# An added one-column memset as VectorE's first instruction, in a streaming multiply and GELU

## The chip, the cores and the metric

One core of one Trainium2 chip runs the kernel. The metric is the device time in microseconds (us), the median of several executions. The profile has a span as well: the time from the first to the last of the program's own instructions in one profiled execution. Time and span are not the same number, and both are given below. The engines are VectorE (DVE in the profile), ScalarE (ACT), GpSimd (POOL), SyncE (SP) and TensorE (PE, which has no work here). Transfers between HBM and the on-chip memory are issued by SP, ACT or POOL and carried out by 16 DMA engines.

## The reference

```python
batch, dim = 1024, 4096          # x and y: float32
z = x * y
out = 0.5 * z * (1 + np.tanh(np.sqrt(2 / np.pi) * (z + 0.044715 * z ** 3)))   # float32
```

Two inputs of 16.8 MB are read, and one output of 16.8 MB is written. Each element is multiplied once and goes through one GELU in its tanh form.

## The kernel before

The arrays are taken as one flat run of 4,194,304 numbers, laid out over 128 partitions, so that each partition has 32,768 columns. `PIECES` cuts the columns into three pieces: 1,280, 16,384 and 15,104 of them. Each piece is contiguous in HBM.

All of x stays in the buffer `xs` (128 x 32,768), where the product and then the GELU overwrite it in place. y goes through a smaller buffer `ys` of 20,440 columns. The y pieces are loaded in the order of `Y_LOADS`: the second piece to column 4,056 of `ys`, then the third to column 0, then the first to column 15,104. The last two overwrite columns that the multiplies of the first have read.

The program is written out by hand, engine by engine, with semaphores. Nothing schedules it.

- SP issues the load of the first x piece (L73), waits for it, then issues the first y load (L77) and the third x piece. The second y load waits for three multiplies (and for the semaphore of the 68-byte load, below), the third for four. Then SP issues the three stores (L124), each when the last GELU of its piece is done, waits for them, and clears the semaphores (L126 to L130).
- ACT issues the load of the second x piece (L73), and then runs one GELU (L115) behind each multiply.
- VectorE runs the multiplies (L107): four of 4,096 columns, seven of 2,048, one of 768 and one of 1,280. The first waits for the first y load and the second x piece (L104).
- GpSimd issues one small load (L83): 17 numbers, 68 bytes, of y to columns 0 to 16 of `ys` in partition 0. They are overwritten by the second y load before anything reads them.

Ahead of these instructions every program has a start stage, which the kernel's framework writes (L145 in the profile): GpSimd fills four constants of one column each with a MEMSET, every engine drains, and a barrier gathers the engines before it releases them. Two more barriers follow (L60). The function `_hoist` takes an instruction from where it was issued and puts it ahead of the start stage of its own engine, in front of that engine's first drain or memset:

```python
    at = next(
        k
        for k, i in enumerate(first)
        if i.engine == engine and type(i).__name__ in ("InstDrain", "InstMemset")
    )
    first[at:at] = issued
```

Three instructions are hoisted: the first x load on SP, the second x load on ACT, and the 68-byte load on GpSimd. So these three stand in front of the first barrier; GpSimd's stands in front of the four constants too. VectorE's first instruction is its drain.

Of the kernel before, what the change touches and what calls it, by code (L numbers as in the profile page):

```python
# [1 line left out]

# [4 lines left out]


F32 = mybir.dt.float32
GELU = mybir.ActivationFunctionType.Gelu_apprx_tanh  # L10

PIECES = [(0, 1280), (1280, 17664), (17664, 32768)]

Y_LOADS = [(1280, 17664, 4056), (17664, 32768, 0), (0, 1280, 15104)]

Y_FREE = [0, 3, 4]

STEPS = [[4096] * 4, [2048] * 7 + [768], [1280]]  # L20
STORES = [(1280, 17664), (17664, 32768), (0, 1280)]
Y_BUF = 20440
SPARE = 0


def _hoist(nc, issued):

    here = nc.cur_bb.bb.instructions
    first = nc.main_func.blocks[0].instructions
    for ins in issued:  # L30
        del here[next(k for k, i in enumerate(here) if i is ins or i.name == ins.name)]
    engine = issued[0].engine
# [8 lines that stand above are left out]
@with_exitstack  # L41
def kernel(
    ctx: ExitStack,
    tc: tile.TileContext,
    x: bass.AP,
    y: bass.AP,
    out: bass.AP,
):
    nc = tc.nc
    P = nc.NUM_PARTITIONS  # L50

    def columns(t, a, b):

        flat = t.flatten_outer_dims().rearrange("r c -> (r c)")
        pa, pb = next(q for q in PIECES if q[0] <= a and b <= q[1])
        return flat[P * pa : P * pb].rearrange("(p c) -> p c", p=P)[:, a - pa : b - pa]


    tc.close()
    tc.compile()  # L60

    xs = nc.alloc_sbuf_tensor("xs", [P, PIECES[-1][1]], F32).ap()
    ys = nc.alloc_sbuf_tensor("ys", [P, Y_BUF], F32).ap()
    sem_x = [nc.alloc_semaphore(f"sem_x{i}") for i in range(len(PIECES))]
    sem_y = [nc.alloc_semaphore(f"sem_y{i}") for i in range(len(Y_LOADS))]
    sem_s = nc.alloc_semaphore("sem_s")
    sem_mul = nc.alloc_semaphore("sem_mul")
    sem_act = nc.alloc_semaphore("sem_act")
    sem_o = [nc.alloc_semaphore(f"sem_o{i}") for i in range(len(STORES))]

    def load_x(i, engine=nc.sync):
        a, b = PIECES[i]
        return engine.dma_start(out=xs[:, a:b], in_=columns(x, a, b)).then_inc(sem_x[i], 16)  # L73

    def load_y(i):
        a, b, r = Y_LOADS[i]
        return nc.sync.dma_start(  # L77
            out=ys[:, r : r + b - a], in_=columns(y, a, b)
        ).then_inc(sem_y[i], 16)

    _hoist(nc, [load_x(0).ins])
    _hoist(nc, [load_x(1, nc.scalar).ins])
    spare = nc.gpsimd.dma_start(  # L83
        out=ys[0:1, SPARE : SPARE + 17], in_=columns(y, 0, 17)[0:1, :]
    ).then_inc(sem_s, 16)
    _hoist(nc, [spare.ins])
    nc.sync.wait_ge(sem_x[0], 16)
    load_y(0)
    load_x(2)
    for i in range(1, len(Y_LOADS)):  # L90
        if Y_FREE[i]:
            nc.sync.wait_ge(sem_mul, Y_FREE[i])
        if i == 1:
            nc.sync.wait_ge(sem_s, 16)
        load_y(i)

    nc.scalar.wait_ge(sem_x[0], 16)
    n = 0
    done = {}
    for i, (a, b, r) in enumerate(Y_LOADS):  # L100
        for j, (xa, xb) in enumerate(PIECES):
            if xa <= a < xb:
                nc.vector.wait_ge(sem_x[j], 16)
        nc.vector.wait_ge(sem_y[i], 16)  # L104
        c = a
        for w in STEPS[i]:
            nc.vector.tensor_mul(  # L107
                out=xs[:, c : c + w],
                in0=xs[:, c : c + w],
                in1=ys[:, r + c - a : r + c - a + w],  # L110
            ).then_inc(sem_mul, 1)
            n += 1
            done[c + w] = n
            nc.scalar.wait_ge(sem_mul, n)
            nc.scalar.activation(  # L115
                out=xs[:, c : c + w], in_=xs[:, c : c + w], func=GELU
            ).then_inc(sem_act, 1)
            c += w

    for i, (a, b) in enumerate(STORES):  # L120
        if i == 0:
            nc.sync.wait_ge(sem_y[-2], 16)
        nc.sync.wait_ge(sem_act, done[b])
        nc.sync.dma_start(out=columns(out, a, b), in_=xs[:, a:b]).then_inc(sem_o[i], 16)  # L124
    for i in range(len(STORES) - 1):
        nc.sync.wait_ge(sem_o[i], 16)  # L126
    nums = sorted(s.num for s in [*sem_x, *sem_y, *sem_o[:-1], sem_s, sem_mul, sem_act])
    assert nums == list(range(nums[0], nums[-1] + 1))
    nc.sync.sem_clear(range(nums[0], nums[-1] + 1))
    nc.sync.wait_ge(sem_o[-1], 16).then_inc(sem_o[-1], -16)  # L130


# [1 line left out]
_INS = ['x', 'y']  # L134
_OUTS = [((1024, 4096), 'float32')]


# [23 lines left out]
```

## Time and profile before

| what | value |
|---|---|
| time, median of 3 runs | 119.35 us (119.30 to 119.42) |
| time of the profiled execution | 119.36 us |
| span of the profiled execution | 118.5 us |
| VectorE busy | 35.2 us, 13 instructions |
| ScalarE busy | 30.9 us, 14 instructions |
| GpSimd busy | 0.8 us, 5 instructions |
| moved by DMA | 50.33 MB, mean 425 GB/s over the span |
| VectorE's first multiply starts | 42.68 us |
| the 68-byte load, from issue to landing | 10.0 us |

Zero of all profile times is the span's start, which is the start of SP's first load. The page gives each engine's busy time, and the same in 40 equal slices as tenths, with the share of the DMA engines below. The chain that ended last is followed back from the last instruction to what released it, step by step. A timeline row gives start, length, engine, source line, operation and output<-input. A "q" behind an engine's name marks its sequencer, which waits, drains and issues transfers; such rows are not counted as busy time. The one DMA issue that counts as busy is GpSimd's.

### The profile page before, as it was taken

How to read it: one execution, taken by the hardware profiler on the slowest of the kernel's cores; microseconds unless marked ns; L12 is line 12 of the kernel's file. 1: busy time of each engine (PE TensorE's matmuls, PEld its weight loads, DVE VectorE, ACT ScalarE, POOL GpSimd, SP SyncE). 2: the span in 40 equal slices, each digit the busy share in tenths (PEclk: the TensorE clock that was granted, in tenths of full speed). 3: DMA queues.
4: the chain of work that ended last, by engine and by line, in shares of the span. 5: the costliest groups of instructions: out<-in, count | busy, mean ns of one | idle time of the engine just before them, and what ended most of it. 6: DMA issues, size and time to landing. Idle time of an engine off the chain costs nothing.

```text
span 118.5 us, 85 instructions
## 1 busy us (share of the span) xinstructions
DVE 35.2 (30%) x13; ACT 30.9 (26%) x14; POOL 0.8 (1%) x5
## 2 busy tenths in 40 slices
DVE  0000000000000059999920000059999940000000
ACT  0000000000000000999975000006998990000000
POOL 2000000000000000000000000000000000000000
DMA  9888899889988897798797797798899887977975
GB/s 464 381 382 382 381 553 509 354 354 420 641 354 354 354 632 347 326 632 347 326 632 347 326 632 347 326 575 354 354 531 531 354 354 326 652 326 326 652 326 221
DMA packets 1328, 50.33 MB, mean 425 GB/s; under 512 B 176, under 2 KB 176, under 8 KB 560
## 3 DMA queue, kind: packets, MB, share of 16 engines
q1 hardware_dynamic: 1152, 41.94, 82.2%
q10 hardware_dynamic: 144, 8.39, 16.6%
q0 software_dynamic: 32, 0.00, 0.0%
HBM read 33.55 MB, written 16.78 MB: 425 GB/s over the span
## 4 chain that ended last, share of the span: by engine, by line
DMA 55%; DVE 24%; ACT 3%; issue 1%; DVEq 0%
DMA ys<-in_y_dram 41%; DVE xs L107 24%; DMA xs<-in_x_dram 13%; ACT xs L115 3%; DVEq L104 0%
## 5 line engine op out<-in xcount | busy, mean ns | idle before, releaser
L107 DVE TENSOR_TENSOR xs<-xs,ys 128x2048 f32<-128x2048 f32 (+3 forms) x13 | 35.2, 2778 | 60.9 <-DMA ys<-in_y_dram 60.9
L115 ACT ACTIVATE xs<-xs 128x2048 f32<-128x2048 f32 (+3 forms) x13 | 29.6, 2300 | 19.6 <-DVE xs L107 19.6
L115 ACT ACT_TABLE_LOAD x1 | 1.3, 1283 | 47.2 <-DVE xs L107 47.2
L83 POOL DMA_DIRECT2D ys<-in_y_dram x1 | 0.6, 632 | 0.7 <-issue 0.7
L145 POOL MEMSET const-bfloat16-1.0<- 128x1 bf16 x1 | 0.1, 130 | 0.0
L145 POOL MEMSET const-uint8-127<- 128x1 uint8 x1 | 0.1, 130 | 0.0
L145 POOL MEMSET const-float32-0.0<- 128x1 f32 x1 | 0.1, 128 | 0.0
L145 POOL MEMSET const-float32-1.0<- 128x1 f32 x1 | 0.1, 127 | 0.0
## 6 DMA issues: line engine op xcount, KB each, us to landing
xs<-in_x_dram SPq DMA_DIRECT2D x1, 7552.0 KB, 44.0
ys<-in_y_dram SPq DMA_DIRECT2D x1, 7552.0 KB, 22.5
out_dram<-xs SPq DMA_DIRECT2D x1, 7552.0 KB, 20.4
xs<-in_x_dram SPq DMA_DIRECT2D x1, 640.0 KB, 16.0
ys<-in_y_dram SPq DMA_DIRECT2D x1, 640.0 KB, 19.7
out_dram<-xs SPq DMA_DIRECT2D x1, 640.0 KB, 20.8
xs<-in_x_dram ACTq DMA_DIRECT2D x1, 28.0
ys<-in_y_dram POOLq DMA_DIRECT2D x1, 0.1 KB, 10.0
```

Source lines behind the costliest of these rows:

```text
L83: spare = nc.gpsimd.dma_start(out=ys[0:1, SPARE : SPARE + 17], in_=columns(y, 0, 17)[0:1, :]).then_inc(sem_s, 16)
L107: nc.vector.tensor_mul(out=xs[:, c : c + w], in0=xs[:, c : c + w], in1=ys[:, r + c - a : r + c - a + w],).then_inc(sem_mul, 1)
L115: nc.scalar.activation(out=xs[:, c : c + w], in_=xs[:, c : c + w], func=GELU).then_inc(sem_act, 1)
L145: nc = _bacc.Bacc("TRN2", target_bir_lowering=False, num_devices=1)
```

## The change

One constant and one line are added. VectorE gets a memset of column 32 of `ys` (128 partitions, one float32 each, value 0), hoisted to the front of VectorE's instructions, ahead of its first drain. Column 32 is not among the columns 0 to 16 of the 68-byte load, and the second y load overwrites it before a multiply reads it. All other engines keep their instructions and the order of them; GpSimd's first is still the 68-byte load. The two added lines shift the line numbers by one or two.

```diff
 Y_BUF = 20440
+EARLY = 32
 SPARE = 0
...
+    _hoist(nc, [nc.vector.memset(ys[:, EARLY : EARLY + 1], 0.0).ins])
     _hoist(nc, [load_x(0).ins])
     _hoist(nc, [load_x(1, nc.scalar).ins])
     spare = nc.gpsimd.dma_start(
```

## The prediction

> **What bounds the kernel now.** I read the page first (busy shares and the 40 slices), then the chain that ended last, then the timeline of the first two microseconds, then the rows of the line that holds the start barrier. All times below are microseconds from the start of the span unless a duration is meant.
>
> The slices of the page (busy tenths by engine, then the share of the 16 DMA engines):
>
> ```profile
> span 118.5 us, 85 instructions
> DVE  0000000000000059999920000059999940000000
> ACT  0000000000000000999975000006998990000000
> POOL 2000000000000000000000000000000000000000
> DMA  9888899889988897798797797798899887977975
> ```
>
> The reader is to see that DMA is busy from the first slice to the last, while VectorE (DVE) works in two islands, and does nothing at all in the first 14 slices. The kernel is a stream of 50.33 MB through the DMA engines. Its interior can only change if the transfers start later, or if a transfer is held back.
>
> The chain that ended last (start, length, what) begins with three transfers or waits on transfers:
>
> ```profile
> 0.00 15.99 DMA xs<-in_x_dram
> 15.99 0.02 issue
> 16.01 26.57 DMA ys<-in_y_dram
> ```
>
> So the first row on which anything depends is SP's load at 0.00, and nothing else of the first 15.99 us is on the path. VectorE's first multiply follows at 42.68, when the large y load has landed.
>
> The timeline of the start (start, length, engine, line, operation):
>
> ```profile
> 0.00 0.39 SPq L73 DMA_DIRECT2D xs<-in_x_dram  x1
> 0.12 0.36 ACTq L73 DMA_DIRECT2D xs<-in_x_dram  x1
> 0.74 0.63 POOL L83 DMA_DIRECT2D ys<-in_y_dram  x1 [0.74 <-issue]
> 1.35 0.13 POOL L145 MEMSET const-float32-0.0<- 128x1 f32 x1
> 1.39 0.13 POOL L145 MEMSET const-float32-1.0<- 128x1 f32 x1
> 1.42 0.13 POOL L145 MEMSET const-bfloat16-1.0<- 128x1 bf16 x1
> 1.46 0.13 POOL L145 MEMSET const-uint8-127<- 128x1 uint8 x1
> ```
>
> The reader is to see that three DMA issues stand before the first instruction in which a compute engine writes anything: GpSimd's MEMSET at 1.35 (1.355 in the trace). VectorE has no row here.
>
> And the barrier that ends this stage, in the rows of line 145 (ns min/median/max, first and last start):
>
> ```profile
> L145 DVEq DRAIN  x1: 10/10/10, 0.1 to 0.1; - x1
> L145 POOLq DRAIN  x1: 10013/10013/10013, 0.8 to 0.8; - x1
> ```
>
> VectorE reaches the barrier at 0.12 and stands there until GpSimd's drain, 10.01 long, ends at 10.83.
>
> **The clock's own ends.** The profiled execution has a time of 119.36, its span is 118.53. The time is 0.83 longer, so it isn't the span, and where it begins has to be inferred. If it begins at t, it ends at 119.36 + t. The trace has semaphore records behind the span: resets of single semaphores from 118.80 to 119.41, then a chain of nine hand-offs around the engines from 119.63 to 119.99. A clock that began with SP's load at 0.00 would end at 119.36, in the middle of the resets, where no engine has just finished. A clock that began with GpSimd's DMA row (0.738) would end at 120.10, which is 0.11 behind the last hand-off. One that began with GpSimd's first MEMSET (1.355) would end at 120.715, which is 0.73 behind it. I take the last. DMA_DIRECT2D is the same operation in the first three rows, so a rule by which it opens the clock would have opened it at 0.00; the first row that is certainly work of a compute engine is the MEMSET.
>
> The Trainium skill bears on both ends. Its page "Perfetto Trace Analysis" (section "GPSIMD Engine Instruction") says that a GpSimd instruction that reads no tensor has no reported start, so that 0.738 may not be a start at all; no run here shows it. Its page "Runtime: NRT & Kernel Launch" (section "The ~15µs preamble/postamble breakdown") lists, behind the kernel, a barrier, semaphore resets and a second barrier with a re-arming of the DMA rings, some 5 us in sum; by that figure the end would be an estimated 123.5 and the start 4.2, where nothing of the first rows begins, and the trace's resets, 0.61 long against its 1.5, disagree with it.
>
> **The change part by part.** It adds one instruction, VectorE's memset of one column (128x1 f32) of ys. It removes and moves nothing: the other four engines have the same instructions in the same order, and SP's and ACT's loads are still the first of their queues.
>
> - Its own work: the nearest row is GpSimd's MEMSET of 128x1 f32, 0.13. VectorE has no work before 42.68, so it costs nothing there.
> - VectorE's arrival at the barrier: its DRAIN now stands behind the memset. It would be late by some 0.07 to start and 0.13 to run, so at about 0.32 in place of 0.12. The barrier is gathered at 10.87, behind GpSimd's 10.01 drain: 10.5 of slack. Without that cover the 0.2 would go to the next wait, SP's for x piece 0 from 11.67 to 15.99, which hides 4.3 more. Cost nothing.
> - Transfers: column 32 lies outside the 68-byte load (columns 0 to 16) and is written next by the y load issued at 55.80. No wait is added, and nothing queues behind the memset but the barrier. Cost nothing.
> - GpSimd: whether a VectorE memset can hold up GpSimd's rows isn't in the trace. Between 0 and one memset, 0.13; I take 0. The Trainium skill's page "SBUF — State Buffer" (section "Who interferes with whom") says that a VectorE instruction with at most one SBUF input, outside its two-port modes, doesn't contend with GpSimd; no run here shows it, and the sum is the same by it.
> - The clock's start: this is the only term. The memset becomes the first row in which a compute engine writes. Earliest start: VectorE's sequencer has its first record, the DRAIN, at 0.119. Latest: GpSimd's first record is at 0.137 and its first instruction at 0.738, 0.60 later, so 0.119 + 0.60 = 0.72. The nearest row is VectorE's own: from its wait at 42.605 to its multiply at 42.676, 0.07. I take 0.119 + 0.07 = 0.19. The clock opens at 0.19 in place of 1.355: 1.165 more, with bounds of 1.355 - 0.72 = 0.64 and 1.355 - 0.12 = 1.24.
>
> The sum against the profiled execution: 119.36 + 0 + 0 + 0 + 1.165 = 120.525. That execution stands 0.01 above the median of the three runs (119.35), so the forecast for the median is 120.51. No work takes longer; the time counts 1.17 us of loading that it didn't count before. 0.2% is 0.24 us, about what a measurement of this kernel can tell from no change (the three runs lie 0.12 apart).
>
> **The rivals.**
>
> *The clock begins with GpSimd's DMA row.* Then it opened at 0.738 before and opens at 0.19 now: 0.55 more, 119.90 (0.02 to 0.62 by the same bounds of the memset's start). For it: the page counts this row as busy time of GpSimd, as it does not with SP's and ACT's, and an end only 0.11 behind the last hand-off needs no unseen work. Against it: the operation has the same name on all three engines.
>
> *The clock doesn't begin with a compute engine's first write.* It begins at SP's load at 0.00, or at something ahead of the program, and a memset that starts at 0.12 or later comes behind it. All other terms are nothing, so the time stays at 119.35 plus or minus 0.06. This is also the case in which the instruction is added but counts for nothing. For it: the span itself begins at SP's row, and 0.83 could be work ahead of the span, of which the trace has some (semaphore hand-offs from -0.37 to 0.00, small transfers from -0.77). Against it: an end at 119.36 falls between two resets. It decides as soon as the clock's start is at or before 0.12.
>
> *The memset holds up GpSimd, and only GpSimd's rows open the clock.* GpSimd's first row would be late by up to 0.13, and the clock would open that much later, so the time would be 119.22. For it: both engines start within 0.02 of each other (0.119 and 0.137). Against it: a rule that counts GpSimd's MEMSET and not VectorE's is odd, and no row shows such a wait. It is below the 0.24 that counts as faster; to be faster, the hold would have to last two memsets or more.
>
> **How the numbers follow.** The forecast gets 0.60: of GpSimd's two rows on which the 119.36 can be placed, the MEMSET is the one that the operation's name favours, and an end among the resets is the worst fit. The DMA row gets 0.20, of which 0.02 lies in the low end of its bounds, under 0.24. A start that doesn't move gets 0.12 and the held GpSimd 0.04, half of it beyond 0.24. The last 0.04 is left for a gap that no row of before shows, half slower and half faster. So slower is 0.60 + 0.18 + 0.02 = 0.80, same 0.12 + 0.02 + 0.02 = 0.16, faster 0.02 + 0.02 = 0.04. The range holds the forecast and the first rival, all but its low end, which is 8 in 10 once the forecast's bounds are in it: from 119.90 less the runs' half spread of 0.06, 119.84, to 119.35 + 1.24 + 0.06 = 120.65.
>
> **What would show it.** In the profile of after: a DVE MEMSET row near 0.2, 0.1 to 0.15 long; the other rows of the start, the chain, and the span (118.5) as before; and the time less the span at about 2.0 in place of 0.83. Growth of the time with an unchanged span shows the clock; the memset's start taken from the old start gives which row opened it: 1.355 if the growth is near 1.2, 0.738 if it is near 0.55. A time of 119.3 to 119.4 with the memset at 0.2 would refute the forecast. So would a longer span: then the memset delayed a transfer, and the place to look is the first x load's landing, 15.99 now.

## The result, and the profile after

The changed kernel takes 119.80 us (median of 5 runs, 119.75 to 119.81) against 119.30 (119.26 to 119.42) for the kernel before beside it. The ratio is 1.0039, with a 95% interval of 1.0025 to 1.0054. A second comparison, further below, gave 119.95 against 119.36, a ratio of 1.0046 (1.0032 to 1.0060). So it is slower, by 0.5 to 0.6 us. The forecast was 120.51; what came is 0.4 to 0.5 of the growth that it gave, and close to what the first rival gave (119.90).

The page of the changed kernel, its span and the slices:

```profile
span 118.3 us, 86 instructions
DVE  0000000000000069999920000059999940000000
ACT  0000000000000001999974000006998990000000
POOL 2000000000000000000000000000000000000000
DMA  9888899889988897797797797798899887977975
```

The reader is to see one more instruction and a span that has not grown: 118.331 by the trace, 118.533 before. The profiled execution has a time of 119.75. Time less span is 1.419 in place of 0.827, which is 0.592 more. In this pair of executions all of the loss, and more, lies outside the span.

The timeline of the first two microseconds, without its last three rows (the other constants):

```profile
0.00 0.38 SPq L74 DMA_DIRECT2D xs<-in_x_dram  x1
0.12 0.36 ACTq L74 DMA_DIRECT2D xs<-in_x_dram  x1
0.15 0.06 DVE L82 MEMSET ys<- 128x1 f32 x1
0.73 0.63 POOL L85 DMA_DIRECT2D ys<-in_y_dram  x1 [0.73 <-issue]
1.34 0.13 POOL L147 MEMSET const-float32-0.0<- 128x1 f32 x1
```

The memset starts at 0.147 and takes 0.059; the other rows are within 0.02 of where they were. Now the two numbers meet: 0.738, the start of GpSimd's load row before, less 0.147 is 0.591, and time less span grew by 0.592. The last semaphore hand-off behind the span says the same. It came at 119.990 before and at 119.789 here. A clock that opened at 0.738 before closed at 120.098, and one that opened at 0.147 here closed at 119.897: both 0.108 behind the hand-off. The 0.108 follows from taking these rows as the opening; what two executions can show is that opening and close moved together. With the forecast's opening at 1.355, the close would have moved from 0.725 behind it to 0.108.

The barrier's rows confirm the cover that the prediction named:

```profile
L147 DVEq DRAIN  x1: 77/77/77, 0.2 to 0.2; - x1
L147 POOLq DRAIN  x1: 10002/10002/10002, 0.8 to 0.8; - x1
```

VectorE's drain grew from 10 to 77 ns, and its arrival moved from 0.140 to 0.245. GpSimd's drain of 10.00 us still ends the stage.

One thing in the chain looks like an effect of the change and is none:

```profile
0.00 13.35 DMA xs<-in_x_dram
13.35 0.02 issue
13.37 29.02 DMA ys<-in_y_dram
```

The first x load lands at 13.35, not 15.99, while the y load behind it takes 29.02, not 26.57. The repeat of the changed kernel shows the other landing (its chain, first and third row of the same view):

```profile
0.00 16.08 DMA xs<-in_x_dram
...
16.09 26.59 DMA ys<-in_y_dram
```

Both landings occur with many of the kernels below (13.35 to 13.65, or 15.99 to 16.14), and the sum of the two rows stays between 42.4 and 42.7. So what the first load gains, the next one loses. The profiled spans are 118.3 to 118.6 with the early landing and 118.5 to 118.7 with the late one; in 35 runs of the kernel before on one chip they lay between 118.4 and 118.8.

### The profile page after: what moved, and what is told of

Its sections match the earlier page's. It is cut to its first block, busy times and chain, and to the rows that moved or that the text cites. A ratio compares the mean times of both kernels' runs of the same rounds, so it can differ in the third digit from the quotient of the medians.

```text
span 118.3 us, 86 instructions
## 1 busy us (share of the span) xinstructions
DVE 35.3 (30%) x14; ACT 30.9 (26%) x14; POOL 0.8 (1%) x5
## 4 chain that ended last, share of the span: by engine, by line
DMA 55%; DVE 24%; ACT 3%; issue 1%; DVEq 0%
DMA ys<-in_y_dram 44%; DVE xs L109 24%; DMA xs<-in_x_dram 11%; ACT xs L117 3%; DVEq L106 0%
```

## The experiments

The theory, called *first row*: the clock opens at the earliest row of work on a compute engine, GpSimd's load row counted, and closes 0.108 behind the last hand-off. Then time less span is 0.827 + 0.738 - opening, so the opening is 1.565 less (time less span). Spans are taken from the trace to the nanosecond, times are given to 0.01, so an opening is good to some 10 ns. The close is as steady as that: the last hand-off stands 1.451 to 1.458 behind the end of the span in the traces of all the kernels here. The runs show differences: that the clock opens at the very start of a row, and closes 0.108 behind the hand-off, is the choice that sets the formula, and a common offset at both ends would fit as well. The rivals were *constants* (the forecast: GpSimd's first MEMSET opened it) and *added work* (the instruction itself delays something).

The diffs are against the changed kernel where they touch its memset, and against the kernel before otherwise. Lines that allocate the semaphore `sem_e` and clear it at the end are left out, and so is the constant `EARLY`.

**The memset late.**

```diff
-    _hoist(nc, [nc.vector.memset(ys[:, EARLY : EARLY + 1], 0.0).ins])
...
+    wait = nc.vector.wait_ge(sem_s, 16)
+    _hoist(nc, [wait.ins, nc.vector.memset(ys[:, EARLY : EARLY + 1], 0.0).ins])
```

> The changed kernel, but VectorE waits for the 68-byte load's landing (about 10.7 us) ahead of the added memset. Theory, first row: the clock opens at the earliest row of work on VectorE, ScalarE or GpSimd, GpSimd's load row counted, and closes a fixed 0.11 us behind the last hand-off; time less span is 1.565 minus that start. The load's row at 0.74 is first again, so time less span is 0.83 and the time is that of the kernel before, 119.3. Rival, constants (the forecast): the clock opened at GpSimd's first MEMSET, 1.355; the memset is now behind it, so the time is also 119.3. Rival, added work: one more VectorE instruction in front of the barrier costs about 0.5 wherever it starts, so 119.8; this run tells it from the other two.

The time was 119.29 against 119.31, ratio 0.9994 (0.9986 to 1.0003). The memset's row:

```profile
10.73 0.06 DVE L89 MEMSET ys<- 128x1 f32 x1 [10.73 <-DMA ys<-in_y_dram]
```

Same instruction, still in front of the barrier, and no cost. Added work falls: what costs is when the memset starts.

**The memset in between.**

```diff
-    _hoist(nc, [nc.vector.memset(ys[:, EARLY : EARLY + 1], 0.0).ins])
-    _hoist(nc, [load_x(0).ins])
+    _hoist(nc, [load_x(0).ins, nc.sync.sem_inc(sem_e).ins])
+    wait = nc.vector.wait_ge(sem_e, 1)
+    _hoist(nc, [wait.ins, nc.vector.memset(ys[:, EARLY : EARLY + 1], 0.0).ins])
```

> The changed kernel, but VectorE waits for a semaphore that SP raises behind its first load, so that the one-column memset starts at about 0.5, between 0.15 and the 68-byte load's 0.74. First row: time less span is 1.565 minus the memset's start, about 1.07, and the growth over the kernel before is about 0.24 (119.55), half of that of the changed kernel. Constants: 1.355 minus 0.5 over the kernel before, 0.85 (120.15). Added work: 119.8 as for the changed kernel.

The time was 119.56, ratio 1.0015 (1.0006 to 1.0023).

```profile
0.49 0.06 DVE L85 MEMSET ys<- 128x1 f32 x1 [0.49 <-SPq L83]
0.73 0.63 POOL L87 DMA_DIRECT2D ys<-in_y_dram  x1 [0.73 <-issue]
```

Time less span was 1.075, so the opening is 0.490, and the row starts at 0.490. The growth is 0.25 by the medians (0.07 to 0.27 by the interval), where constants asked for 0.85. The forecast's reading falls here.

**GpSimd's load later, first attempt.**

```diff
-    _hoist(nc, [load_x(0).ins])
+    _hoist(nc, [load_x(0).ins, nc.sync.sem_inc(sem_e).ins])
...
+    wait = nc.gpsimd.wait_ge(sem_e, 1)
+    _hoist(nc, [wait.ins])
     _hoist(nc, [spare.ins])
```

> The kernel before, without a VectorE memset; GpSimd waits, ahead of the 68-byte load, for a semaphore that SP raises behind its first load (about 0.4). All GpSimd rows start later by 0.2 to 0.4, at about 1.0 for the load and 1.6 for the first constant. No transfer on the path changes. First row: the clock opens 0.2 to 0.4 later, time less span falls to 0.4 to 0.6 and the time to about 119.0, with no work done sooner. Constants: the same fall, since both rows move. Start at SP's load or ahead of it: no change, 119.3.

119.34, ratio 0.9999 (0.9990 to 1.0007). This tells nothing about the clock, because the edit didn't move the row: the load was expected at about 1.0 and stood at 0.737. SP raised the semaphore at 0.442. Behind a wait the load's row starts 0.29 to 0.30 after the release, here and in the three later runs that have such a wait (0.674 to 0.966, 0.675 to 0.967, 1.272 to 1.567), so this release was too early to move it. It was done again with a later semaphore, below.

**The constants first.**

```diff
-    _hoist(nc, [spare.ins])
+    _hoist(nc, [spare.ins], ("InstDrain",))
```

> The kernel before, without a VectorE memset, but GpSimd's four constants come ahead of the 68-byte load. First row: the clock opens at the first constant. If GpSimd's first instruction takes 0.6 to begin whatever it is, that is 0.74 and nothing changes (119.3); if the 0.6 belongs to the load, the constant starts at about 0.2, time less span is about 1.36 and the time 119.85. Constants (opening at 1.355 before): with the constant at 0.2 the time would be 120.4, with it at 0.74 119.9.

119.77, ratio 1.0039 (1.0024 to 1.0054). The changed kernel's loss comes back without any memset on VectorE.

```profile
0.25 0.09 POOL L145 MEMSET const-float32-0.0<- 128x1 f32 x1 [0.25 <-issue]
...
0.84 0.63 POOL L83 DMA_DIRECT2D ys<-in_y_dram  x1 [0.40 <-issue]
```

Time less span was 1.315: an opening at 0.250, against 0.246 for the row. So a constant opens the clock as well if it comes first, and half a microsecond earlier than the load did. The 0.6 between GpSimd's first record and its first row belongs to the load, not to whatever instruction is first.

**A wide memset.**

```diff
-    _hoist(nc, [nc.vector.memset(ys[:, EARLY : EARLY + 1], 0.0).ins])
+    _hoist(nc, [nc.vector.memset(ys[:, EARLY : EARLY + 1024], 0.0).ins])
```

> The changed kernel with a memset of 1024 columns in place of one, so about 1 us long, started at the same 0.15. First row: only the start counts, so time less span is 1.42 and the time is that of the changed kernel, 119.8. Constants: the same. Added work: the cost grows with the work, by about 1 us, to 120.8, if it is the work; the barrier's 10 us wait for GpSimd covers it otherwise.

Here the theory missed, and so did all rivals: 119.39 against 119.31, ratio 1.0002 (0.9993 to 1.0010).

```profile
0.36 0.91 DVE L82 MEMSET ys<- 128x1024 f32 x1 [0.36 <-issue]
0.74 0.63 POOL L85 DMA_DIRECT2D ys<-in_y_dram  x1 [0.74 <-issue]
```

The row stands at 0.36, well ahead of the load's, and yet time less span is 0.818, an opening at 0.747. A thousand columns cost nothing where one costs 0.5. Seven of the runs that follow ask why.

*The value.*

```diff
-    _hoist(nc, [nc.vector.memset(ys[:, EARLY : EARLY + 1], 0.0).ins])
+    _hoist(nc, [nc.vector.memset(ys[:, EARLY : EARLY + 1024], 1.0).ins])
```

> The 1024-column memset with the value 1 in place of 0. If a fill with zeros is what isn't counted, the row at 0.36 opens the clock now and time less span is 1.2 (119.7); if the size decides, it stays at 0.82 (119.35).

119.28, ratio 0.9997 (0.9987 to 1.0006), time less span 0.842. It isn't the zeros.

*A ladder of sizes.*

```diff
-    _hoist(nc, [nc.vector.memset(ys[:, EARLY : EARLY + 1], 0.0).ins])
+    at, ladder = EARLY, []
+    for n in (256, 64, 16, 4, 1):
+        ladder.append(nc.vector.memset(ys[:, at : at + n], 0.0).ins)
+        at += n
+    _hoist(nc, ladder)
```

> The 1024-column memset had a row at 0.361 and yet time less span stayed at 0.82, which by the first-row theory means an opening at 0.74. Here VectorE's first instructions are five memsets in a row, of 256, 64, 16, 4 and 1 columns, so that the time tells which of them opens the clock: 1.565 minus time less span is the opening. First row as it stood: the 256-column one, at about 0.15 to 0.36, so time less span is 1.2 to 1.4. First row with a limit on the memset's size: the first one under the limit, with later starts (about 0.5 to 0.74) and time less span of 0.83 to 1.07. Constants: dead after the half-microsecond step of the 1-column memset.

119.89, ratio 1.0051 (1.0034 to 1.0067), time less span 1.366: an opening at 0.199, and the 256-column row starts at 0.201. So 256 columns count.

*GpSimd's load behind the wide memset.* The memset raises a semaphore at its end, and GpSimd waits for it.

```diff
-    _hoist(nc, [nc.vector.memset(ys[:, EARLY : EARLY + 1], 0.0).ins])
+    fill = nc.vector.memset(ys[:, EARLY : EARLY + 1024], 0.0).then_inc(sem_e, 1)
+    _hoist(nc, [fill.ins])
...
+    wait = nc.gpsimd.wait_ge(sem_e, 1)
+    _hoist(nc, [wait.ins])
     _hoist(nc, [spare.ins])
```

> The 1024-column memset is VectorE's first instruction as before, and GpSimd waits for its end (about 1.3) ahead of the 68-byte load, so that GpSimd's rows all come later: the load at 1.4 to 1.9, the constants 0.62 behind it. No transfer on the path changes. Wide memset not counted, GpSimd's load row opens the clock: time less span is 1.565 minus that row's start, 0.2 or below zero, and the time falls to 118.2 to 118.7, though no work is done sooner. Wide memset counted after all and the 0.82 due to something else: 0.36 opens, time less span 1.2, time 119.7. Opening at a fixed point of the start stage: no change, 119.3.

119.70, ratio 1.0035 (1.0022 to 1.0048).

```profile
0.36 0.91 DVE L83 MEMSET ys<- 128x1024 f32 x1 [0.36 <-issue]
1.57 0.63 POOL L87 DMA_DIRECT2D ys<-in_y_dram  x1 [1.57 <-DVE ys L83]
```

Time less span is 1.204, an opening at 0.361: the same memset, at the same 0.36, now opens the clock. Two things differ from the wide memset alone, the semaphore and the place of the load.

*The semaphore alone.* As above, without GpSimd's wait.

```diff
-    _hoist(nc, [nc.vector.memset(ys[:, EARLY : EARLY + 1], 0.0).ins])
+    fill = nc.vector.memset(ys[:, EARLY : EARLY + 1024], 0.0).then_inc(sem_e, 1)
+    _hoist(nc, [fill.ins])
```

> The changed kernel with a 1024-column memset that raises a semaphore at its end, for which nobody waits; GpSimd's load stays at about 0.73. With GpSimd's load at 1.57 the same memset, with the semaphore, opened the clock at 0.36; without the semaphore and with the load at 0.74 it did not. Order of the ends: a row counts as first by when it ends, and the 1.27 end of this memset is behind GpSimd's load row at 0.73, so the load opens, time less span 0.83 (119.3). Semaphore: a long memset counts only if it signals its end, so 0.36 opens, time less span 1.2 (119.7).

119.36, ratio 1.0000 (0.9990 to 1.0010), time less span 0.827. It isn't the semaphore; it is the place of the load.

*448 and 640 columns.*

```diff
-    _hoist(nc, [nc.vector.memset(ys[:, EARLY : EARLY + 1], 0.0).ins])
+    _hoist(nc, [nc.vector.memset(ys[:, EARLY : EARLY + 448], 0.0).ins])
```

and the same with `EARLY + 640`.

> The changed kernel with a memset of 448 columns, which ends at about 0.68, ahead of GpSimd's load row at 0.73. Order of the ends: the memset is first, its row's start (about 0.25) opens, time less span about 1.3. A limit on the size between 256 and 1024 columns, at or below 448: the load opens, 0.83.

> The changed kernel with a memset of 640 columns, which ends at about 0.87, behind the start of GpSimd's load row (0.73) and ahead of that row's end (1.36). Order of the ends, the load taken at its row's start: the load opens, time less span 0.83. The load taken at a later point of its row, up to 1.27: the memset opens at about 0.3, time less span about 1.27. A limit on the size above 640: the memset opens as well.

With 448 columns: 119.96, ratio 1.0044 (1.0029 to 1.0059), opening 0.237. With 640: 119.40, ratio 0.9999 (0.9989 to 1.0009), opening 0.725. The rows, 448 first:

```profile
0.24 0.43 DVE L82 MEMSET ys<- 128x448 f32 x1 [0.24 <-issue]
0.73 0.63 POOL L85 DMA_DIRECT2D ys<-in_y_dram  x1 [0.73 <-issue]
```

```profile
0.28 0.59 DVE L82 MEMSET ys<- 128x640 f32 x1 [0.28 <-issue]
0.73 0.63 POOL L85 DMA_DIRECT2D ys<-in_y_dram  x1 [0.73 <-issue]
```

The first ends at 0.673, ahead of the load's start; the second at 0.872, behind it. The first counts and the second doesn't.

**The changed kernel once more**, without an edit.

> The changed kernel once more, beside the kernel before on this chip. The opening moves by 0.59 (0.738 to 0.147), but the median rose by 0.50 and the spans were 118.3 to 118.4 against 118.4 to 118.8 in 35 runs before. If the memset shortens the span by 0.1, the spans are 118.3 to 118.4 again and the time is 119.80. If that was scatter from run to run, the spans are around 118.5 and the time is 119.9. Time less span is 1.41 to 1.43 in both cases.

119.95 against 119.36, ratio 1.0046 (1.0032 to 1.0060), time less span 1.408, spans of 118.4 to 118.6. So the shorter spans of the first five runs (118.3 to 118.4) don't come with the memset, and beside spans like those of the kernel before the growth is 0.59.

**The load's row moved, alone and with 640 columns.** ScalarE raises the semaphore behind its load, at the end of a drain.

```diff
-    _hoist(nc, [load_x(1, nc.scalar).ins])
+    x1 = load_x(1, nc.scalar)
+    _hoist(nc, [x1.ins, nc.scalar.drain().then_inc(sem_e, 1).ins])
...
+    wait = nc.gpsimd.wait_ge(sem_e, 1)
+    _hoist(nc, [wait.ins])
     _hoist(nc, [spare.ins])
```

> The kernel before, without a VectorE memset; GpSimd waits, ahead of the 68-byte load, for a semaphore that ScalarE raises at about 0.68, so that the load's row moves to about 0.95 and the constants to about 1.6. No transfer on the path changes and no work is done sooner. First row: the clock opens with the load's row, time less span falls to 1.565 - 0.95 = 0.6, and the time by 0.2, to about 119.1. A fixed point of the start stage near 0.74: no change, 0.83 and 119.35.

119.06 against 119.34, ratio 0.9976 (0.9967 to 0.9985).

```profile
0.97 0.63 POOL L85 DMA_DIRECT2D ys<-in_y_dram  x1 [0.97 <-ACTq L84]
```

Time less span is 0.597, an opening at 0.968, and the row starts at 0.966. The clock follows the load's row. This is below both kernels, but it is no faster kernel: its profiled span is 118.66, and no load or store lands sooner. The clock merely starts later.

Then the same beside the memset of 640 columns:

```diff
+    _hoist(nc, [nc.vector.memset(ys[:, EARLY : EARLY + 640], 0.0).ins])
```

> The 640-column memset of the changed kernel's variant (row 0.28 to 0.87), which did not open the clock with the load's row at 0.73; here the load's row is moved to about 0.95 by the same wait. Order of the ends: the memset now ends ahead of the load's row, so it opens at 0.28, time less span 1.285 and time 119.8. A limit on the size between 448 and 640 columns: the load's row opens, time less span 0.6 and time 119.1.

119.90, ratio 1.0043 (1.0028 to 1.0059).

```profile
0.28 0.59 DVE L83 MEMSET ys<- 128x640 f32 x1 [0.28 <-issue]
0.97 0.63 POOL L87 DMA_DIRECT2D ys<-in_y_dram  x1 [0.97 <-ACTq L86]
```

Time less span is 1.280, an opening at 0.285 against 0.280 for the memset's row. The same 640 columns that didn't count with the load at 0.73 count with the load at 0.97. A limit on the size falls; order of the ends holds in every run.

The theory, mended: a VectorE memset opens the clock, at its row's start, if its row ends ahead of the start of GpSimd's load row; otherwise that load row opens it. (A GpSimd constant that comes ahead of the load opens it too.) The openings worked out from time less span, beside the start of the row that this rule names (us):

| kernel | VectorE memset, start to end | GpSimd's first row | time less span | opening | row named |
|---|---|---|---|---|---|
| before | none | 0.738 | 0.827 | 0.738 (set) | 0.738 load |
| changed | 0.147 to 0.206 | 0.726 | 1.419 | 0.146 | 0.147 memset |
| changed, again | 0.147 to 0.206 | 0.732 | 1.408 | 0.157 | 0.147 memset |
| memset late | 10.727 to 10.786 | 0.729 | 0.840 | 0.725 | 0.729 load |
| memset in between | 0.490 to 0.549 | 0.728 | 1.075 | 0.490 | 0.490 memset |
| constants first | none | 0.246 | 1.315 | 0.250 | 0.246 constant |
| 256 columns, then less | 0.201 to 0.473 | 0.733 | 1.366 | 0.199 | 0.201 memset |
| 448 columns | 0.241 to 0.673 | 0.733 | 1.328 | 0.237 | 0.241 memset |
| 640 columns | 0.280 to 0.872 | 0.731 | 0.840 | 0.725 | 0.731 load |
| 640, load moved | 0.280 to 0.872 | 0.967 | 1.280 | 0.285 | 0.280 memset |
| 1024 columns | 0.361 to 1.273 | 0.738 | 0.818 | 0.747 | 0.738 load |
| 1024, load behind | 0.360 to 1.272 | 1.567 | 1.204 | 0.361 | 0.360 memset |
| load moved | none | 0.966 | 0.597 | 0.968 | 0.966 load |

Three kernels are left out of the table, and fit it: with the value 1, with the semaphore alone and with the load's first attempt the openings are 0.723, 0.738 and 0.744, and the load's rows start at 0.722, 0.732 and 0.737.

Why a long row must end first isn't shown. A clock that takes the start of the row that is recorded first, VectorE's at its end and GpSimd's load as it is issued, would do this; the runs bound the load's own point only between 0.673 and 0.872, with its row at 0.73, so "the start of the load's row" is exact only within that. No run has a row of ScalarE's work at the start, so whether one would count is open.

## Why the prediction was right or wrong

**The step that failed** is the one in "The clock's own ends" that chose between GpSimd's two rows. It took the first constant, at 1.355, on the argument that DMA_DIRECT2D is the same operation on SP, ScalarE and GpSimd, so that a rule which counts it would have opened the clock at 0.00. The runs showed that the name doesn't decide: SP's and ScalarE's issues, at 0.00 and 0.12 in every run, never opened the clock, and GpSimd's did, within 10 ns, wherever it was put (0.72 to 0.74, and 0.966), unless a counted row came ahead of it. Whether it is the engine or the kind of queue isn't separated: the page lists the queue of GpSimd's load as software_dynamic, those of the others as hardware_dynamic. The page before had hinted at the difference. It counts GpSimd's issue as 0.6 of busy time in its groups and leaves the other two out, which the prediction noted, and put under the rival.

**The fit of the close** had the right answer in it. An end 0.11 behind the last hand-off needed no unseen work, one 0.73 behind it did. The prediction had both numbers and gave the second the larger weight. The prediction's caution came from the Trainium skill's page "Perfetto Trace Analysis" (section "GPSIMD Engine Instruction"): a GpSimd instruction that reads no tensor has no reported start. Here the measurement decides against it: the start of the load's row and the clock's opening moved together by 0.23. The caution couldn't have chosen between the two rows anyway, since the MEMSET reads no tensor either.

**What held.** The only term is the clock's start: memset late and memset in between show that directly. No wait or barrier moved the time, and no transfer's landing followed the memset: VectorE's arrival at 0.245 stays 10 us ahead of GpSimd's drain. The memset holds up nothing on GpSimd: its load row stayed at 0.72 to 0.74 beside every memset that it didn't wait for, 1024 columns included. This agrees with the Trainium skill's page "SBUF — State Buffer" (section "Who interferes with whom"), by which a VectorE instruction with at most one SBUF input, outside the two-port modes, doesn't contend with GpSimd. The memset's start was forecast at 0.19 with bounds of 0.12 to 0.72, and came at 0.147; its length was taken from GpSimd's row, 0.13, and came at 0.059. With the right row, the sum gives 0.55 by the forecast's start and 0.59 by the measured one; measured were 0.50 and 0.59.

**The rivals.** The load's row: confirmed. A clock that doesn't begin with a compute engine: refuted, since the opening follows such rows in both directions. GpSimd held up: refuted. The range reached down to 119.84 only because it took in the rival of the load's row; the first median lay 0.04 below that, the second inside, so the second is no credit to the forecast's mechanism. That rival's low bound should have carried the scatter of the span, 0.1 to 0.3 from run to run, not half the spread of three runs.

## What to carry to other kernels

Where time and span differ, work out the opening and the close first: take one row as the opening, add the time, and see whether the close lands on something that the trace shows, then ask which candidate needs the least unseen. In a program whose first loads are hoisted ahead of its start stage, an early memset on an idle VectorE can cost as much as its head start over the row that opened the clock, though it delays nothing; whether ScalarE's work would do the same wasn't run. And a time that falls because the first counted row comes later is no speed: compare spans and landings as well.

## What the runs showed of the hardware

The start of a VectorE memset's row moves with its width. VectorE's sequencer reaches the drain behind the memset at 0.158 to 0.159 whatever the width, but the rows of 1, 448, 640 and 1024 columns start at 0.147, 0.241, 0.280 and 0.361 and end at 0.206, 0.673, 0.872 and 1.273. The ends are 1.04 ns a column apart (1.067 over 1,023 columns), the starts 0.21 ns a column. If the engine begins at the same moment for every width, which no run shows directly, the row leaves out about a fifth of the work.

GpSimd's MEMSET of one column begins 0.11 behind its sequencer's first record when it comes first (0.138 to 0.246). Behind the 68-byte load it begins at 1.355, 0.62 behind the load row's start, and it stayed 0.62 behind it wherever the load stood. With the 68-byte load in front of it, beside the large x loads, GpSimd's drain took 9.4 to 10.2 us.
